# Block 2's feed-forward, first product: seven block products in place of eight for pairs of output blocks

## The chip, the cores and the metric

The kernel runs on one core of one Trainium2 chip. The metric is device time in microseconds (us) of one execution, as a median over several runs. Engines are named as the profile names them: PE is TensorE's matmul, PEld its weight load, DVE is VectorE, ACT is ScalarE, POOL is GpSimd, SP is SyncE, on whose queue the weight loads are issued.

## The reference

Two transformer blocks over 512 tokens of width 1024, in float32. The second has two layers, and each ends in this feed-forward; the change touches nothing else:

```python
D_MODEL = 1024
SEQ = 512
DEPTH_2 = 2
D_FF_2 = 4 * D_MODEL
...
        h = rmsnorm(x, mlp_norm[l])
        u = jnp.square(jax.nn.relu(jnp.einsum('bsd,df->bsf', h, w_ff1[l])))
        x = x + jnp.einsum('bsf,fd->bsd', u, w_ff2[l])
```

## The kernel before

Everything is kept feature-major: a tile has 128 features on its partitions and the 512 tokens along its row. The residual stream is eight such tiles, X0 to X7. To get float32 accuracy from PE's faster fp32r mode, each operand is split into a rounded part (hi, made by an ACT cast) and the rest (lo, made by a DVE subtraction), and each product is three matmuls: hi·hi, lo·hi and hi·lo (`mm3`). A weight block of 128 x 1024 numbers is loaded by one DMA into a raw buffer (`load_w`, a ring of three), then split into a hi and a lo tile (rings of two).

A layer's feed-forward has eight chunks (ch = 0 to 7). A chunk has two stages. Stage ff1 makes four blocks of 128 hidden features: each is 8 contraction steps x 3 = 24 matmuls of 512 columns into a bank of PSUM, and `emit_relu2` then takes it from the bank with DVE (relu and scale), squares it on ACT, and splits it into u hi and lo. Stage ff2 multiplies the four u tiles by four weight blocks; each gives two output tiles of 12 matmuls, which DVE adds to X (`add_residual`, X0 to X7 in order). Both stages take their banks from a ring of two ("mm"), so a group of matmuls cannot begin before DVE has taken the group two before it out of its bank. The 32 blocks that the change speaks of are a layer's 8 chunks x 4 blocks.

Each engine executes its instructions in the order in which they stand in its queue. That order is made when the program is built: a list scheduler goes by priorities, and `tc.high_priority(offset=...)` moves a weight load and its split ahead of other work, by 250 (LOOKAHEAD) before. An instruction that waits holds up all that stand behind it on its engine.

Names in the trace: L0 and L1 are block 2's layers; L1wf_r, L1wf_h and L1wf_l are the raw, hi and lo weight tiles of both stages, L1wf_p their banks, L1m the normed input, L1u the hidden tiles, L1rl the relu tiles, and fin is the last ff2 of the kernel, which `finish` runs in two token halves of 256 columns.

Of the kernel before, what the change touches and what calls it, by code (L numbers as in the profile page):

```python
# [10 lines left out]
F32 = mybir.dt.float32  # L11
F32R = mybir.dt.float32r
# [3 lines left out]
AF = mybir.ActivationFunctionType  # L16
ALU = mybir.AluOpType
# [39 lines left out]
def _f(t):  # L57
    return t.bitcast(F32)
# [125 lines left out]
def transformer_kernel(ctx: ExitStack, tc: tile.TileContext, d, out):  # L184
    nc = tc.nc
# [82 lines left out]
    C = {n: packed[:, c] for n, c in PACK.items()}  # L268
# [69 lines left out]
    def split(x, name):  # L338

        hi, lo = act_pair(name)  # L340
        S.copy(hi, x)
        V.tensor_tensor(lo, x, _f(hi), ALU.subtract)
        return hi, lo

    def normed(gain, name):

        h = []
        for k in range(KT):
            hi, lo = act_pair(f"{name}{k}")
# [13 lines left out]
    def load_w(src, name, tags=None):  # L363

        kt, cols = src.shape[1], src.shape[2]
        n = kt * cols
        raw = early.pop(len(warm), None) if len(warm) < 2 else None
        load = raw is None
        if load:
            raw = wp.tile([P, 1120], F32, tag="raw", name=name + "_r", bufs=3)  # L370
        warm.append(True)
        if tags:
            hi, lo = (pair(t, name + t, F32R).rearrange("p a b -> p (a b)") for t in tags)
        else:
            hi = wp.tile([P, 1120], F32R, tag="hi", name=name + "_h", bufs=2)
            lo = wp.tile([P, 1120], F32R, tag="lo", name=name + "_l", bufs=2)
        clock.take()
        with tc.high_priority(offset=LOOKAHEAD):
            if load:
                nc.sync.dma_start(raw[:, :n], src.rearrange("p k c -> p (k c)"))  # L380
            for c in (slice(0, n),) if load else (slice(0, n // 2), slice(n // 2, n)):
                S.copy(hi[:, c], raw[:, c])  # L382
                V.tensor_tensor(lo[:, c], raw[:, c], _f(hi)[:, c], ALU.subtract)  # L383
        clock.take(background=True)
        return (hi[:, :n].rearrange("p (k c) -> p k c", c=cols), lo[:, :n].rearrange("p (k c) -> p k c", c=cols))

    def mm3(ps, lh, ll, rh, rl, start, stop):
        TE.matmul(ps, lh, rh, start=start, stop=False)  # L388
        TE.matmul(ps, ll, rh, start=False, stop=False)  # L389
        TE.matmul(ps, lh, rl, start=False, stop=stop)  # L390

    def spare(n, name):

        if "s" in pool:
            return [bank("s", f"{name}_{i}") for i in range(n)]
        return [two_banks(f"{name}_{i}")[:, 0] for i in range(n)]

    def gemm_fm(src, h, emit, name, m0=0, banks=()):

        kt, cols = src.shape[2], src.shape[3]  # L400
        banks = list(banks)
        for b in range(src.shape[0]):
            wh, wl = load_w(src[b], f"{name}_{b}")
            for m in range(cols // P):
                ps = banks.pop(0) if banks else bank("mm", f"{name}_p{b}_{m}")
                c = slice(m * P, (m + 1) * P)
                for k in range(kt):
                    mm3(ps, wh[:, k, c], wl[:, k, c], h[k][0], h[k][1], k == 0, k == kt - 1)
                    if k % 2 == 1 and k < kt - 1:
                        yield True  # L410
                emit(m0 + b * (cols // P) + m, ps)
                yield True
# [38 lines left out]
    def run(gen):  # L451
        for _ in gen:
            pass
# [643 lines left out]
    def layer(l):  # L1097
        L = f"L{l}"
        h = normed(C["attn_norm"][:, l * KT : (l + 1) * KT], L + "h")
# [263 lines left out]
        h3 = normed(C["mlp_norm"][:, l * KT : (l + 1) * KT], L + "m")  # L1363
        rn3, rb3 = stats(L + "st3")
        for ch in range(8):
            u = []

            def emit_relu2(m, ps):
                t = sb("evt", f"{L}rl{ch}{m}")
                V.scalar_tensor_tensor(t, ps, 0.0, rb3, ALU.max, ALU.mult)  # L1370
                S.activation(t, t, AF.Square)
                u.append(split(t, f"{L}u{ch}_{m}"))

            run(gemm_fm(d["w_ff1"][l, 4 * ch : 4 * ch + 4], h3, emit_relu2, f"{L}wf1{ch}", 0, spare(2, L + "spf") if ch == 0 else ()))
            if l == 1 and ch == 7:
                finish(d["w_ff2"][l, ch], u)
            else:
                run(gemm_fm(d["w_ff2"][l, ch], u, add_residual, f"{L}wf2{ch}"))

    def finish(src, u):  # L1380

        w = [load_w(src[b], f"wfin{b}", t) for b, t in enumerate((("pa", "pb"),) * 3 + (("qs", "kh"),))]
        for half in range(2):
            t0 = slice(half * 256, (half + 1) * 256)
            for m in range(KT):
                wh, wl = w[m // 2]
                ps = bank("mm", f"fin{half}{m}")[:, :256]
                c = slice(m % 2 * P, (m % 2 + 1) * P)
                for k in range(4):
                    mm3(ps, wh[:, k, c], wl[:, k, c], u[k][0][:, t0], u[k][1][:, t0], k == 0, k == 3)  # L1390
                with tc.high_priority(offset=LOOKAHEAD):
                    V.tensor_tensor(X[m][:, t0], X[m][:, t0], ps, ALU.add)
            acc = sum_squares(f"stf{half}", t0, half == 1)
            pb = spread(inv_rms(acc, f"stf{half}", D), f"stf{half}")[:, :256]
            for k in range(0, KT, 2):
                o = sb("kA" if half == 0 else "kB", f"fo{half}{k}").rearrange("p (a t) -> p a t", a=2)
                for a in range(2):
                    V.scalar_tensor_tensor(o[:, a], X[k + a][:, t0], C["final_norm"][:, k + a : k + a + 1], pb, ALU.mult, ALU.mult)
                nc.sync.dma_start(out[:, k : k + 2, t0], o)

    for l in range(2):
        layer(l)
# [122 lines left out]
```

## Time and profile before

| what | value |
|---|---|
| time, median of 3 runs | 2021.6 us (2020.47 to 2024.03) |
| the profiled execution's own time | 2021.86 us |
| its span, first to last instruction | 2020.1 us |
| PE busy | 1973.4 us, 98% of the span |
| DVE busy | 1175.5 us, 58% |
| ACT busy | 880.0 us, 44% |
| POOL busy | 44.3 us, 2% |
| mean granted TensorE clock | 0.991 of full speed |

PE is busy nearly throughout, and the chain that ended last runs through it. Matmuls overlap one another, so what a matmul costs is the distance from its start to the next one's start, not its own length.

### The profile page before, as it was taken

The page shows a single profiled execution, that of the slowest core. Times are in us where ns is not written, and L with a number is a line of the kernel's source. Part 1 is how long each engine was busy: PE and PEld are TensorE (multiplying, and loading weights), DVE is VectorE, ACT ScalarE, POOL GpSimd, SP SyncE. Part 2 cuts the span into 40 slices and gives each one's busy share as a digit, 9 for nine tenths or more (in the row PEclk, how much of TensorE's full clock was granted, in tenths as well). Part 3 has the DMA queues.
Part 4 walks back from the last instruction along what each step waited for, and adds up shares of the span by engine and source line. Part 5 has one row for each costly group of instructions (what it writes and reads, how often), then busy time and mean ns, then how long its engine had stood idle before and what let it go on. Part 6 is the DMA issues. An engine that isn't in the chain of part 4 may idle for free.

```text
span 2020.1 us, 25945 instructions
## 1 busy us (share of the span) xinstructions
PE 1973.4 (98%) x10197; PEld 1611.3 (80%) x10197; DVE 1175.5 (58%) x2032; ACT 880.0 (44%) x1494; POOL 44.3 (2%) x87
## 2 busy tenths in 40 slices
PE   8999899999999999999999999999999999999998
PEld 7888766788888878787778888888888778888887
DVE  7685877744444457558764444447466864444446
ACT  6642555522222235587542223335577643322223
POOL 0000000000000000001000000000000000000000
PEclk9998999999999999999999999999999999999999
DMA  5222200122222222212122222223221212222222
GB/s 185 72 76 65 69 27 22 53 94 94 94 94 94 95 96 91 83 42 85 61 84 94 94 98 99 95 94 104 75 68 58 74 63 95 98 99 95 94 94 73
DMA packets 50922, 168.65 MB, mean 83 GB/s; under 512 B 5808, under 2 KB 8240, under 8 KB 50800
## 3 DMA queue, kind: packets, MB, share of 16 engines
q1 hardware_dynamic: 47680, 161.93, 23.4%
q0 software_dynamic: 2976, 4.98, 1.2%
q8 instruction: 81, 1.33, 0.3%
q14 instruction: 41, 0.34, 0.1%
q10 hardware_dynamic: 144, 0.07, 0.0%
HBM read 160.14 MB, written 2.10 MB: 80 GB/s over the span
## 4 chain that ended last, share of the span: by engine, by line
PE 49%; ACT 3%; DVE 1%; issue 1%; DVEq 0%; ACTq 0%
PE L0wf_p L390 6%; PE L0wf_p L388 6%; PE L0wf_p L389 6%; PE L1wf_p L390 5%; PE L1wf_p L388 5%; PE L1wf_p L389 5%; PE L1z L1210 1%; PE L0wo_p L388 1%; PE L1wo_p L388 1%; PE L0wo_p L389 1%; PE L1wo_p L389 1%; PE L0wo_p L390 1%; PE L1wo_p L390 1%; PE L1sbo L1224 1%; PE L1wdf_p L388 0%
## 5 line engine op out<-in xcount | busy, mean ns | idle before, releaser
L382 ACT CAST L0wf_h<-L0wf_r 128x1024 fp32r<-128x1024 f32 x64 | 67.3, 1051 | 229.3 <-PE L0wf_p L390 224.8
L382 ACT CAST L1wf_h<-L1wf_r 128x1024 fp32r<-128x1024 f32 x60 | 63.1, 1051 | 221.0 <-PE L1wf_p L390 216.7
L390 PE MATMUL wgu_p<-h_l,wgu_h 128*128 128x512 f32 x328 | 128.8, 393 | 0.0
L388 PE MATMUL wgu_p<-h_h,wgu_h 128*128 128x512 f32 x328 | 128.7, 392 | 0.0
L389 PE MATMUL wgu_p<-h_h,wgu_l 128*128 128x512 f32 x328 | 128.6, 392 | 0.0
L382 ACT CAST wgu_h<-wgu_r 128x1024 fp32r<-128x1024 f32 x44 | 46.2, 1051 | 168.6 <-issue 65.1
L388 PE MATMUL L0wf_p<-L0u_h,L0wf_h 128*128 128x512 f32 x256 | 100.7, 393 | 0.0
L389 PE MATMUL L0wf_p<-L0u_h,L0wf_l 128*128 128x512 f32 x256 | 100.3, 392 | 0.0
L390 PE MATMUL L0wf_p<-L0u_l,L0wf_h 128*128 128x512 f32 x256 | 99.4, 393 | 0.0
L390 PE MATMUL L0wf_p<-L0m_l,L0wf_h 128*128 128x512 f32 x240 | 94.2, 393 | 0.0
L390 PE MATMUL L1wf_p<-L1m_l,L1wf_h 128*128 128x512 f32 x240 | 94.2, 393 | 0.0
L388 PE MATMUL L0wf_p<-L0m_h,L0wf_h 128*128 128x512 f32 x240 | 94.2, 392 | 0.0
L388 PE MATMUL L1wf_p<-L1m_h,L1wf_h 128*128 128x512 f32 x240 | 94.2, 392 | 0.0
L389 PE MATMUL L0wf_p<-L0m_h,L0wf_l 128*128 128x512 f32 x240 | 94.1, 392 | 0.0
L389 PE MATMUL L1wf_p<-L1m_h,L1wf_l 128*128 128x512 f32 x240 | 94.1, 392 | 0.0
L383 DVE TENSOR_TENSOR L0wf_l<-L0wf_r,L0wf_h 128x1024 fp32r<-128x1024 f32 x64 | 78.4, 1225 | 24.6 <-ACT L0wf_h L382 24.6
L388 PE MATMUL L1wf_p<-L1u_h,L1wf_h 128*128 128x512 f32 x224 | 88.1, 393 | 0.0
L389 PE MATMUL L1wf_p<-L1u_h,L1wf_l 128*128 128x512 f32 x224 | 87.8, 392 | 0.0
L383 DVE TENSOR_TENSOR L1wf_l<-L1wf_r,L1wf_h 128x1024 fp32r<-128x1024 f32 x60 | 73.5, 1225 | 23.3 <-ACT L1wf_h L382 23.3
L390 PE MATMUL L1wf_p<-L1u_l,L1wf_h 128*128 128x512 f32 x224 | 87.0, 393 | 0.0
L456 DVE TENSOR_TENSOR X<-X,L0wf_p 128x512 f32<-128x512 f32 x64 | 44.0, 687 | 67.2 <-PE L0wf_p L390 67.2
L456 DVE TENSOR_TENSOR X<-X,L1wf_p 128x512 f32<-128x512 f32 x56 | 38.5, 688 | 66.6 <-PE L1wf_p L390 66.6
(829 smaller groups left out, 5389.9 us busy)
## 6 DMA issues: line engine op xcount, KB each, us to landing
L0wf_r<-w_ff SPq DMA_DIRECT2D x64, 512.0 KB, 3.2
L1wf_r<-w_ff SPq DMA_DIRECT2D x60, 512.0 KB, 3.3
wgu_r<-w_gu SPq DMA_DIRECT2D x44, 512.0 KB, 3.2
wdn_r<-w_dn SPq DMA_DIRECT2D x22, 512.0 KB, 3.3
wns_r<-w_nsa SPq DMA_DIRECT2D x8, 512.0 KB, 3.6
wout_r<-w_out SPq DMA_DIRECT2D x8, 512.0 KB, 3.3
L0wsb_r<-w_sbqk SPq DMA_DIRECT2D x8, 512.0 KB, 3.2
L0wdf_r<-w_dfqk SPq DMA_DIRECT2D x8, 512.0 KB, 3.2
```

Source lines behind the costliest of these rows:

```text
L382: S.copy(hi[:, c], raw[:, c])
L383: V.tensor_tensor(lo[:, c], raw[:, c], _f(hi)[:, c], ALU.subtract)
L388: TE.matmul(ps, lh, rh, start=start, stop=False)
L389: TE.matmul(ps, ll, rh, start=False, stop=False)
L390: TE.matmul(ps, lh, rl, start=False, stop=stop)
L456: V.tensor_tensor(X[m], X[m], ps, ALU.add)
L1210: TE.matmul(ps[:, g, c0:], lhs, rhs[:, g], start=False, stop=(m == len(terms) - 1), skip_group_check=True)
L1224: TE.matmul(po[g * 64 : (g + 1) * 64, j * P + c0 : j * P + c1], sv[j][:, (2 * i + g) * 64 : (2 * i + g + 1) * 64], e[:, g, c0:c1], start=( ...
```

## The change

In each layer, chunk 0 keeps the plain ff1. In chunks 1 to 7 the four blocks are made as two pairs by `gemm_seven`. A pair's product (256 features x 1024 inputs by 1024 inputs x 512 tokens) is cut in two along each of the three directions, and the two-by-two block product is done with seven block products instead of eight, in Strassen's scheme with Winograd's sums. Each of the seven is 128 features x 512 inputs x 256 tokens: 4 contraction steps x 3 = 12 matmuls of 256 columns. So a pair has 84 matmuls of 256 columns where it had 48 of 512.

The scheme needs sums of operands. Weight sums are made for each pair, on POOL: `s1`, `s2`, `a21` (in place) and `s4`, four additions of 128x512. The seven weight operands are then split one by one (`weight_part`: an ACT cast and a DVE subtraction of 128x512 each), where the pair before had two splits of 128x1024. Their tiles come from twelve slots in rotation, so the sixth operand (f) of a pair lies where the first (a) of the pair before it lay. Token sums are made once for each layer from X (`token_parts`), on DVE and ACT, in chunk 0. The seven products (a to g in the order of the program) share three banks; between them ACT copies and DVE additions of 256 columns combine the results (`x`, `y` and `z` are the tiles xy, u0 and u1). `emit_relu2` then works from SBUF.

```diff
+AHEAD7 = 350
...
             def emit_relu2(m, ps):
-                t = sb("evt", f"{L}rl{ch}{m}")
+                t = ps if ch else sb("evt", f"{L}rl{ch}{m}")
                 V.scalar_tensor_tensor(t, ps, 0.0, rb3, ALU.max, ALU.mult)
                 S.activation(t, t, AF.Square)
                 u.append(split(t, f"{L}u{ch}_{m}"))
 
-            run(gemm_fm(d["w_ff1"][l, 4 * ch : 4 * ch + 4], h3, emit_relu2, f"{L}wf1{ch}", 0, spare(2, L + "spf") if ch == 0 else ()))
+            if ch == 0:
+                run(gemm_fm(d["w_ff1"][l, 0:4], h3, emit_relu2, f"{L}wf1{ch}", 0, spare(2, L + "spf")))
+                parts = token_parts(C["mlp_norm"][:, l * KT : (l + 1) * KT], h3, L)
+            else:
+                for n in (0, 2):
+                    gemm_seven(d["w_ff1"][l, 4 * ch + n : 4 * ch + n + 2], parts, lambda m, t: emit_relu2(n + m, t),
+                               f"{L}w7{ch}{n}", "to"[n // 2])
...
+    slots = [("kA",) * 2, ("kB",) * 2, ("kA",) * 2, ("kB",) * 2, ("h1",) * 2, ("h2",) * 2, ("kG",) * 2,
+             ("pa",), ("h0",), ("pa",), ("h0",), ("pa",)]
+    turn_ = [0]
+
+    def weight_part(x, name):
+        s = slots[turn_[0] % len(slots)]
+        turn_[0] += 1
...
+        S.copy(hi, x)
+        V.tensor_tensor(lo, x, _f(hi), ALU.subtract)
...
+    def token_parts(gain, h, name):
...
+        for k in range(4):
...
+            V.tensor_tensor(t1, a[:, two], a[:, one], ALU.subtract)
+            S.activation(t1, t1, AF.Copy, scale=ga)
+            S.activation(t3, a[:, two], AF.Copy, scale=ga)
+            V.scalar_tensor_tensor(t2, c[:, two], gc, t1, ALU.mult, ALU.subtract)
+            V.scalar_tensor_tensor(t3, c[:, two], gc, t3, ALU.mult, ALU.subtract)
+
+            V.scalar_tensor_tensor(t4, c[:, one], gc, t2, ALU.mult, ALU.subtract)
+            for (hi, lo), t in zip(parts, (t1, t2, t3, t4)):
+                S.copy(hi[:, k], t)
+                V.tensor_tensor(lo[:, k], t, _f(hi)[:, k], ALU.subtract)
...
+    def gemm_seven(src, parts, emit, name, third):
+
+        b11, b21, b22, t1, t2, t3, t4 = parts
+        raw = []
+        with tc.high_priority(offset=AHEAD7):
+            for n in range(2):
+                r = wp.tile([P, 1120], F32, tag="raw", name=f"{name}_r{n}", bufs=3)
+                nc.sync.dma_start(r[:, :1024], src[n].rearrange("p k c -> p (k c)"))
+                raw.append(r)
+            a11, a12, a21, a22 = raw[0][:, 0:T], raw[0][:, T : 2 * T], raw[1][:, 0:T], raw[1][:, T : 2 * T]
+            s12 = pair("kx", name + "_s")
+            s1, s2, s4 = s12[:, 0], s12[:, 1], sb("ho", name + "_s4")
+            G.tensor_tensor(s1, a21, a22, ALU.add)
+            G.tensor_tensor(s2, s1, a11, ALU.subtract)
+            G.tensor_tensor(a21, a11, a21, ALU.subtract)
+            G.tensor_tensor(s4, a12, s2, ALU.subtract)
+            order = (("a", a11, b11), ("b", s2, t2), ("c", s1, t1), ("d", a12, b21), ("e", a21, t3), ("f", s4, b22), ("g", a22, t4))
+            w = [weight_part(x, name + e) for e, x, _ in order]
...
+        def product(i, ps, start):
+            (wh, wl), (bh, bl) = w[i], order[i][2]
+            for k in range(4):
+                for m, (x, y) in enumerate(((wh, bh), (wl, bh), (wh, bl))):
+                    TE.matmul(ps, x[:, k], y[k], start=start and k == 0 and m == 0, stop=k == 3 and m == 2, skip_group_check=True)
+
+        p0, p1, p2 = banks
+        xy, u0, u1 = (sb("evt", f"{name}{e}") for e in "xyz")
+        product(0, p0, True)
+        S.copy(xy[:, one], p0)
+        product(1, p1, True)
+        V.tensor_tensor(xy[:, two], p1, xy[:, one], ALU.add)
+        product(2, p2, True)
+        V.tensor_tensor(u1[:, two], p2, xy[:, two], ALU.add)
+        product(3, p0, False)
+        S.copy(u0[:, one], p0)
+        product(4, p1, True)
+        V.tensor_tensor(u1[:, two], p1, u1[:, two], ALU.add)
+        product(5, p2, False)
+        V.tensor_tensor(u0[:, two], p2, xy[:, two], ALU.add)
+        emit(0, u0)
+        product(6, p1, False)
+        V.tensor_tensor(u1[:, one], p1, xy[:, two], ALU.add)
+        emit(1, u1)
```

The change adds a line at the top, so a line of the helpers above it stands one lower after it (`add_residual` is L456 before and L457 after).

DVE in the ff2 stage of layer 0's chunk 3, where its second and third weight blocks are worked on. Before, each X addition stands right behind the one before it or one split:

```order
L456 TENSOR_TENSOR X2_98<-X2_98,L0wf23_p1_0_9875 128x512
L456 TENSOR_TENSOR X3_99<-X3_99,L0wf23_p1_1_9889 128x512
L383 TENSOR_TENSOR L0wf23_3_l_9939<-L0wf23_3_r_9937,L0wf23_3_h_9938 128x1024
L456 TENSOR_TENSOR X4_100<-X4_100,L0wf23_p2_0_9909 128x512
L456 TENSOR_TENSOR X5_101<-X5_101,L0wf23_p2_1_9923 128x512
L383 TENSOR_TENSOR L0wf14_0_l_9973<-L0wf14_0_r_9971,L0wf14_0_h_9972 128x1024
```

The same place in the changed program. L0w740 is layer 0, chunk 4, the pair that begins with block 0; the letter behind is the operand (a to g), r0 and r1 are the two raw tiles, s the sums s1 and s2, s4 the last sum:

```order
L457 TENSOR_TENSOR X3_99<-X3_99,L0wf23_p1_1_10366 128x512
L384 TENSOR_TENSOR L0wf23_3_l_10416<-L0wf23_3_r_10414,L0wf23_3_h_10415 128x1024
L1402 TENSOR_TENSOR L0w740b_10462<-L0w740_s_10452,L0w740b_10462 128x512
L1402 TENSOR_TENSOR L0w740c_10465<-L0w740_s_10452,L0w740c_10465 128x512
L1402 TENSOR_TENSOR L0w740d_10468<-L0w740_r0_10448,L0w740d_10468 128x512
L1402 TENSOR_TENSOR L0w740e_10471<-L0w740_r1_10450,L0w740e_10471 128x512
L1402 TENSOR_TENSOR L0w740f_10474<-L0w740_s4_10453,L0w740f_10474 128x512
L1402 TENSOR_TENSOR L0w740gl_10478<-L0w740_r1_10450,L0w740gh_10477 128x512
L457 TENSOR_TENSOR X4_100<-X4_100,L0wf23_p2_0_10386 128x512
L1402 TENSOR_TENSOR L0w742al_10600<-L0w742_r0_10589,L0w742ah_10599 128x512
L1402 TENSOR_TENSOR L0w742dl_10612<-L0w742_r0_10589,L0w742dh_10611 128x512
L457 TENSOR_TENSOR X5_101<-X5_101,L0wf23_p2_1_10400 128x512
```

Six subtractions of the next pair's operands now stand ahead of the X4 addition. The second place is the end of the same ff2 stage and the first products of chunk 4. ACT there, in the changed program:

```order
L1401 CAST L0w742eh_10615<-L0w742_r1_10591 128x512
L1401 CAST L0w742fh_10619<-L0w742_s4_10594 128x512
L383 CAST L0wf24_0_h_10735<-L0wf24_0_r_10734 128x1024
L1462 COPY L0w740x_10483<-L0w740_p_10481 128x256
L383 CAST L0wf24_1_h_10769<-L0wf24_1_r_10768 128x1024
L1401 CAST L0w742g_10623<-L0w742_r1_10591 128x512
```

And DVE at that place; the last row combines product c, and the tile `q` is the bank that product f then adds to:

```order
L457 TENSOR_TENSOR X6_102<-X6_102,L0wf23_p3_0_10420 128x512
L384 TENSOR_TENSOR L0wf24_0_l_10736<-L0wf24_0_r_10734,L0wf24_0_h_10735 128x1024
L457 TENSOR_TENSOR X7_103<-X7_103,L0wf23_p3_1_10434 128x512
L1402 TENSOR_TENSOR L0w742fl_10620<-L0w742_s4_10594,L0w742fh_10619 128x512
L384 TENSOR_TENSOR L0wf24_1_l_10770<-L0wf24_1_r_10768,L0wf24_1_h_10769 128x1024
L1464 TENSOR_TENSOR L0w740x_10483<-L0w740_p_10481,L0w740x_10483 128x256
L1402 TENSOR_TENSOR L0w742g_10623<-L0w742_r1_10591,L0w742g_10623 128x512
L1466 TENSOR_TENSOR L0w740z_10485<-L0w740_q_10482,L0w740x_10483 128x256
```

The additions that free the banks of the first products stand behind splits of the second pair and of the next ff2 weights. On PE the scheduler has also moved the first pair's product a, up to its last matmul, ahead of the ff2 group p3_0; the last matmul of it stands behind p3_1.

## Rows read from the trace of the kernel before

**Rows 1.** The page: span and part 1, busy time and share of each engine.
```profile
span 2020.1 us, 25945 instructions
...
PE 1973.4 (98%) x10197; PEld 1611.3 (80%) x10197; DVE 1175.5 (58%) x2032; ACT 880.0 (44%) x1494; POOL 44.3 (2%) x87
```

**Rows 2.** Busy time in one chunk of layer 1: PE, PEld, DVE, ACT, POOL, clock, DMA.
```profile
1722.00:1766.00 44.00, 44.00 (x192) 35.77 (x191) 20.44 (x25) 13.02 (x16) 0.00 (x0) 1.00 0.28 96
```

**Rows 3.** Timeline of layer 1's feed-forward: start us, length us, engine, line [idle before, releaser].
```profile
1901.73 1.05 ACT L382 CAST L1wf_h<-L1wf_r 128x1024 fp32r<-128x1024 f32 x1 [3.41 <-PE L1wf_p L390]
1902.81 1.22 DVE L383 TENSOR_TENSOR L1wf_l<-L1wf_r,L1wf_h 128x1024 fp32r<-128x1024 f32 x1 [0.39 <-ACT L1wf_h L382]
1904.06 5.78 SPq L380 DMA_DIRECT2D L1wf_r<-w_ff  x2
...
1907.18 1.05 ACT L382 CAST L1wf_h<-L1wf_r 128x1024 fp32r<-128x1024 f32 x1 [4.40 <-PE L1wf_p L390]
...
1929.27 1.05 ACT L382 CAST L1wf_h<-L1wf_r 128x1024 fp32r<-128x1024 f32 x1 [3.22 <-PE L1wf_p L390]
...
1934.86 1.05 ACT L382 CAST L1wf_h<-L1wf_r 128x1024 fp32r<-128x1024 f32 x1 [3.35 <-PE L1wf_p L390]
```

**Rows 4.** Timeline of PE in fin: the first and last of 84 matmuls of 256 columns.
```profile
1988.24 0.38 PE L388 MATMUL fin<-L1u_h,wfin1pa 128*128 128x256 f32 x1 [0.40 <-DVE X L1392]
...
1998.29 0.28 PE L390 MATMUL fin<-L1u_l,wfin0pa 128*128 128x256 f32 x1
```

**Rows 5.** Groups by line and form, DVE and ACT: count | busy us, mean ns | idle before.
```profile
L342 DVE TENSOR_TENSOR L0u_l<-L0rl,L0u_h 128x512 fp32r<-128x512 f32 x32 | 22.2, 693 | 0.0
...
L383 DVE TENSOR_TENSOR L0wf_l<-L0wf_r,L0wf_h 128x1024 fp32r<-128x1024 f32 x64 | 78.4, 1225 | 24.6 <-ACT L0wf_h L382 24.6
...
L1392 DVE TENSOR_TENSOR X<-X,fin 128x256 f32<-128x256 f32 x16 | 6.6, 419 | 2.3 <-PE fin L390 1.7
...
L341 ACT CAST L0u_h<-L0rl 128x512 fp32r<-128x512 f32 x32 | 19.9, 622 | 1.0
...
L320 ACT ACTIVATE stf_sq<-X 128x256 f32<-128x256 f32 x14 | 5.8, 418 | 14.6 <-DVE X L1392 13.3 <-DVE stf_acc L323 1.3
```

**Rows 6.** Timeline of DVE: two independent additions back to back.
```profile
965.26 0.69 DVE L1155 TENSOR_TENSOR L0rt<-L0wdf_p,L0cr 128x512 f32<-128x512 f32 x1 [0.52 <-ACT L0rr L1153]
965.87 0.68 DVE L1156 TENSOR_TENSOR L0rr<-L0rr,L0sr 128x512 f32<-128x512 f32 x1
```

**Rows 7.** The page's part 6: weight loads, KB each, median us to landing.
```profile
L0wf_r<-w_ff SPq DMA_DIRECT2D x64, 512.0 KB, 3.2
```

**Rows 8.** All of POOL's casts (L548): shortest, median and longest ns, starts, forms.
```profile
L548 POOL CAST lev_mask<-lm x5: 608/708/1052, 17.3 to 21.3; 128x512 uint8<-128x512 f32 x4, 128x256 uint8<-128x256 f32 x1
```

**Rows 9.** Timeline of POOL: its last two casts together, and the second alone.
```profile
20.61 1.51 POOL L548 CAST lev_mask<-lm 128x512 uint8<-128x512 f32 x2 [1.16 <-DMA lm<-lev_mask]
...
21.27 0.85 POOL L548 CAST lev_mask<-lm 128x256 uint8<-128x256 f32 x1
```

**Rows 10.** Timeline of DVE at the same place, and the same operations without POOL.
```profile
14.79 0.68 DVE L323 TENSOR_TENSOR st_acc<-st_acc,st_sq 128x512 f32<-128x512 f32 x1
15.39 0.15 DVE L553 TENSOR_TENSOR lbm<-packed 128x4 f32<-128x4 f32 x1
...
20.76 1.10 DVE L323 TENSOR_TENSOR st_acc<-st_acc,st_sq 128x512 f32<-128x512 f32 x1
21.78 0.35 DVE L558 TENSOR_TENSOR lbs<-lbe 128x4 f32<-128x4 f32 x1
```

**Rows 11.** Busy time by stretch around a wait of PE; the clock is third from the end.
```profile
1003.50:1006.70 3.20, 0.16 (x2) 0.00 (x0) 1.99 (x10) 0.78 (x4) 0.00 (x0) 0.98 0.00 0
1006.70:1010.10 3.40, 2.47 (x7) 1.88 (x8) 0.76 (x2) 0.69 (x1) 0.00 (x0) 0.50 0.02 5
1010.10:1013.50 3.40, 3.05 (x8) 1.90 (x7) 2.02 (x3) 1.82 (x3) 0.00 (x0) 0.52 0.00 0
```

More of the change, by code (lines that the diff above doesn't have):

```diff
@@ L1378, in layer @@
                 run(gemm_fm(d["w_ff2"][l, ch], u, add_residual, f"{L}wf2{ch}"))
+    slots = [("kA",) * 2, ("kB",) * 2, ("kA",) * 2, ("kB",) * 2, ("h1",) * 2, ("h2",) * 2, ("kG",) * 2,
[4 more added lines that the diff above has]
+        turn_[0] += 1
+        if len(s) == 1:
+            t = pair(s[0], name, F32R)
+            hi, lo = t[:, 0], t[:, 1]
+        else:
+            hi, lo = (pool["gp"].tile([P, T], F32R, tag=g, name=name + e, bufs=rings[g]) for g, e in zip(s, "hl"))
+        S.copy(hi, x)
+        V.tensor_tensor(lo, x, _f(hi), ALU.subtract)
+        return [z.rearrange("p (k c) -> p k c", c=P) for z in (hi, lo)]
@@ new lines, in token_parts @@
+    def token_parts(gain, h, name):
+        one, two = slice(0, T // 2), slice(T // 2, T)
+        tags = ("qs", "kh", "kl", "pb")
+        parts = [[pair(g, f"{name}T{g}{e}", F32R).rearrange("p a (b t) -> p (a b) t", t=T // 2) for e in "hl"] for g in tags]
+        for k in range(4):
+            a, c = X[k], X[k + 4]
+            ga, gc = gain[:, k : k + 1], gain[:, k + 4 : k + 5]
+            w = sb("evt", f"{name}w{k}")
+            w2 = sb("evt", f"{name}v{k}")
+            t1, t2, t3, t4 = w[:, one], w[:, two], w2[:, one], w2[:, two]
+            V.tensor_tensor(t1, a[:, two], a[:, one], ALU.subtract)
[7 more added lines that the diff above has]
+                V.tensor_tensor(lo[:, k], t, _f(hi)[:, k], ALU.subtract)
+        b11 = [[h[k][e][:, one] for k in range(4)] for e in range(2)]
+        b21 = [[h[k + 4][e][:, one] for k in range(4)] for e in range(2)]
+        b22 = [[h[k + 4][e][:, two] for k in range(4)] for e in range(2)]
+        return [b11, b21, b22] + [[[z[:, k] for k in range(4)] for z in p] for p in parts]
@@ new lines, in gemm_seven @@
+    def gemm_seven(src, parts, emit, name, third):
[15 more added lines that the diff above has]
+            w = [weight_part(x, name + e) for e, x, _ in order]
+        one, two = slice(0, T // 2), slice(T // 2, T)
+        pp = pool["p"].tile([P, 2, T], F32, tag="b", name=name + "_p")
+        banks = [pp[:, 0, one], pp[:, 1, one], bank(third, name + "_q")[:, one]]
+        def product(i, ps, start):
[21 more added lines that the diff above has]
+        emit(1, u1)
```

## The prediction

> **What bounds the kernel now.** I read the page first: PE is busy 98% of the span, POOL 2% [rows 1]. Then busy time by stretch, one chunk of a feed-forward at a time: PE is busy in all 44.00 us at full clock, DVE in 20.44, ACT in 13.02, POOL not at all [rows 2]. So in these stages PE sets the pace, and DVE and ACT wait for it: their splits end waits of 3 to 4 us for PE [rows 3]. What counts is then PE's matmul spacing, and whether the other engines can keep ahead of PE once they have more to do.
>
> Spacing comes from starts that PE releases. In ff2 two casts released by PE, 24 matmuls apart, start at 1901.73 and 1907.18: 5.45/24 = 0.227 us for 512 columns. In ff1 they start at 1929.27 and 1934.86: 5.59/24 = 0.233 [rows 3]. For 256 columns with the same three-matmul pattern, fin shows 84 matmuls, as many as a pair now has, from 1988.24 to 1998.29: 10.05/83 = 0.121 [rows 4].
>
> **What PE saves.** A chunk's ff1 was 96 x 0.233 = 22.36 us; it becomes 2 x 84 x 0.121 = 20.33. The saving is 2.0 us a chunk, 14 chunks: 28 us. It is less than the eighth of the columns (2.8 us a chunk), since 0.121 is more than half of 0.233. Weight loads grow from 48 to 84 a pair; in fin they stood beside 256-column matmuls at that spacing, so they are in the price. Break-even is 2.0 us of new PE waiting a chunk.
>
> **What the others gain in work.** A 128x512 DVE operation takes 0.69 us until its result is seen, and 0.61 from start to start [rows 6]; a 128x1024 split 1.22, a 256-column one 0.42; an ACT cast of 512 takes 0.62, of 1024 1.05 [rows 3, 5], and 256 columns 0.42 [rows 5]. In a chunk DVE loses four 1.22 splits and four relu operations of 0.69, and gains 14 operand splits and four relu operations of 0.69 and ten additions of 0.42: 20.4 - 4.9 + 9.7 + 4.2 = 29.4 us of some 42. ACT goes from 13.0 to 13.0 - 4.2 + 14 x 0.62 + 4 x 0.42 = 19.2. Both would fit on average. POOL gets eight additions a chunk.
>
> What an addition of two 128x512 operands costs on POOL no row shows. The nearest is its cast of one such operand, 0.61 us at the shortest [rows 8]. I bound it by 0.61 below (a second operand costs nothing) and 1.2 above (it costs as much again), and take 0.9, the middle, since nothing in the trace says which end is nearer. As a price from the Trainium skill alone: "GPSIMD Engine Reference", the section on performance versus the Vector engine, has 4497 ns for 2048 columns, an estimate of 1.1 us for 512, by which the sum below would come to some 2095; no row here shows it.
>
> POOL and DVE hinder each other. At 20.76 a DVE addition with both inputs in SBUF took 1.10 us instead of 0.68, and one of four columns at 21.78 took 0.35 instead of 0.15 [rows 10]. POOL's casts ran from 20.61 to 21.27 and 21.27 to 22.12 [rows 9]. The long addition ends at 21.86, 0.59 after the first cast; the half-size cast, which took longer than a full one, ends 0.26 after that; the small addition ends with it, at 22.13. Each waited for the one that had come first. The Trainium skill states this as a rule ("SBUF — State Buffer", the section on SBUF's two separate sides): a DVE operation with two SBUF inputs and a GpSimd operation that reads SBUF exclude each other for the whole instruction. These rows agree. It speaks against this change, which puts 8 POOL additions among DVE's splits. I take additions to X, with one input in PSUM, as not held up; no row shows it.
>
> **The first wait: X4.** I count from the first matmul of an ff2 stage (layer 0, chunk 3 into 4). Its blocks end at 5.5, 10.9 and 16.35 (24 x 0.227 each). The third block's cast can start only when PE frees the first block's hi tile, as in [rows 3]: 5.5 to 6.55; its DVE split runs 6.6 to 7.8 and frees the raw buffer for r1 of pair 740. The load is issued 0.03 later, as at 1904.06 [rows 3], and lands after 3.2 us [rows 7]: 11.05. Only now can POOL begin, s1 first, then s2, then e, then s4. DVE has the split of the fourth ff2 block (wanted at 12.05), then b, which needs s2 cast by ACT. Taken in turn at 0.9: s1 11.1-12.0, s2 12.05-12.95, the split 12.95-14.15, e 14.15-15.05, b 15.05-15.75, s4 15.7-16.6; c starts at 16.6, d 17.2, e 17.85, f 18.45, g 19.05, and X4 19.65 to 20.35. But X4 must empty the bank that PE's group p3_0 uses. PE wants it at 16.35 + 11 x 0.121 (product a, moved there as cover) = 17.7. **PE waits 2.7 us.** With 0.61 the same sequence gives X4 done at 19.25 and 1.55 us; with 1.2, 21.55 and 3.85.
>
> **The second wait: z.** p3_1 then ends at 20.4 + 5.45 = 25.85; call it T. r0 of 740 is free when d's split is done at 17.9, so r1 of 742 lands at 21.15. POOL, again in turn with DVE: s1 21.55-22.45, s2 22.5-23.4, e 24.1-25.0, s4 25.7-26.6. Operand f of 742 lies where 740's a lay, so its cast needs PE's last a matmul, which stands behind p3_1 (T + 0.35), and s4: 26.65-27.3. Queued behind it on ACT are ff2's next first split, 27.3-28.3, and the copy of a, to 28.7. The second of these weight blocks needs r0 of 742 free (s4, 26.6), so it lands at 29.85 and is cast by 30.95. DVE in its order: first split to 29.55, X7 to 30.2, f to 30.8, second split 31.0-32.2, x 32.15-32.55, g 32.5-33.2, z 33.55. Product f may add to its bank only after z. PE gets there after the last a, c, b, d and four matmuls of the next a: T + 41 x 0.121, with some 0.1 of start-up, = 30.75. **PE waits 2.8 us.** Other chunks have another order (five of them with z ahead of g, one with z ahead of the split), so I take 2.3 as the mean; with 0.61 1.5, with 1.2 3.0.
>
> Later additions are on time by the same count (742's own z at 42.7, where PE wants it at 43.4), and the wait of the next ff2 for u stays at the few tenths that it was.
>
> **The sum.** A chunk: 2.7 + 2.3 - 2.0 = +3.0 us, 14 chunks: +42. Token sums: 4 x (5 x 0.42 + 3 x 0.47) = 14 us of DVE a layer in chunk 0, whose cover is DVE's idle 44 - 20.4 = 23.6 us; with the first two pairs' splits (9.7) and POOL's turns (7.2) the demand is 51 of 44, so 0 to 7 us a layer, and I take 3.5: +7. `finish` wants the token sums' buffers for its lo weights, free only after the last product: one to two splits of 1.22, +2. Against the profiled execution's 2021.9 (median of the runs 2021.6): 2021.9 + 42 + 7 + 2 = **2073 us**. With POOL at 0.61 and no cost in chunk 0: 1.55 + 1.5 - 2.0 = 1.05 a chunk, 2037. With 1.2: 4.85 x 14 = 68, 14 and 3: 2107.
>
> **Rivals.**
> *The work is hidden: faster.* If POOL and DVE did not wait for each other here and an addition took 0.61, s4 would be done at 13.7, the six splits would start at 13.3 and X4 be done at 17.65, ahead of PE's 17.7; z would be late by about 1.0 us in the mean. -1.0 x 14 and up to 5 for chunk 0 and the end: some 2010; with z on time too, 1994. For it: both engines have idle time on average. Against it: [rows 9, 10], and the late landing of r1. It decides at 2.0 us of waits a chunk.
> *The clock falls.* PE waited 3.2 us at 1003.5, and the next 6.8 us ran at 0.50 of the clock [rows 11], the 1.2 GHz level. Two waits of 2 to 4 us a chunk are near that. Half clock costs 1.7 us per 3.4; once a chunk, over 3.4 or 6.8 us, 14 x 1.7 to 3.4 = 24 to 48 on top: 2097 to 2121. Against: the waits of 2.7 and 2.3 are shorter.
> *Nothing moves.* Waits of 1.5 to 2.5 us a chunk eat the saving: 2015 to 2029.
>
> **Chances.** My sum (2037 to 2107) 0.50; hidden 0.24; clock falls 0.14; near break-even 0.12, of which 0.07 within 0.2% (about 4 us, what a measurement tells from no change), 0.01 faster and 0.04 slower. So faster 0.25, same 0.07, slower 0.68. The range runs from 2006, well into the hidden case, to 2112; outside are fully hidden work and the worse half of the clock's case. My sum's own range is 2037 to 2107.
>
> **What would show it.** Right: 256-column matmuls at 0.12; in each ff2 a PE wait of 2 to 4 us at p3_0 with an X addition as releaser; a second, released by DVE's z, at product f; L1402 subtractions over 0.69 us in the mean where POOL runs; POOL additions of 0.6 to 1.2 us. Wrong: no idle time of PE at p3_0, or DVE durations unchanged beside POOL (then the hidden case), or granted clock below 1.00 in these chunks.

## The result, and the profile after

The changed kernel takes 2147.4 us (median of 4 runs, 2142.8 to 2151.4); the kernel before, on the same chip, 2021.5. The ratio is 1.0621, with an interval of 1.0608 to 1.0634: slower, as forecast, but 126 us slower instead of 51, and beyond the range. The profiled execution has a span of 2142.7 us, 122.6 more than before.

The head of its page, which answers to [rows 1]: PE is no longer busy all the time, and no other engine is.

```profile
span 2142.7 us, 28834 instructions
PE 2002.7 (93%) x11205; PEld 1665.9 (78%) x11205; DVE 1365.7 (64%) x2376; ACT 974.6 (45%) x1738; POOL 223.6 (10%) x199
```

A window over five chunks of layer 0, from the end of chunk 1's last addition to X to that of chunk 6, first of the kernel before, then of the changed one. Columns: the window, its length, busy time (and number of instructions) of PE, weight loads, DVE, ACT and POOL, then the granted clock, the DMA share and GB/s.

```profile
1120.10:1341.30 221.20, 221.20 (x962) 179.81 (x961) 103.38 (x121) 65.12 (x81) 0.00 (x0) 1.00 0.28 96
```
```profile
1141.70:1400.00 258.30, 228.17 (x1328) 197.94 (x1327) 162.79 (x223) 93.25 (x152) 63.44 (x42) 0.96 0.24 82
```

A chunk took 221.2/5 = 44.2 us and takes 51.7. The two bounds also show the first chunks: chunk 1 ends 21.6 us later than before. In layer 1 the same ends were 1742.0 and 1963.1 and are 1826.9 and 2082.8. So ten chunks in mid-course cost 37.1 + 34.8 = 72 us, the two first chunks of both layers 21.6 + 30.3 = 52 us, and the remaining last chunks and the end come to -1.

What PE waits for, in layer 0 from 1200 to 1400 (engine, tile and line of the waiting matmul, its releaser, us in total, times, longest):

```profile
PE L0wf_p L389 <- DVE X L457: 14.7, 4, 3.9
PE L0w_p L1457 <- ACT L0w760x L1462: 3.1, 1, 3.1
PE L0w_p L1457 <- ACT L0w750x L1462: 2.2, 1, 2.2
```

The first is the predicted wait of p3_0 for X4, once a chunk and 3.7 us long. The chain behind it is the predicted one. POOL's four additions for pair 740, then DVE's subtractions up to X4 (start, us, engine, line):

```profile
1224.35 1.29 POOL L1443 TENSOR_TENSOR L0w_s<-L0w_r 128x512 f32<-128x512 f32 x1 [33.89 <-DMA L0w_r<-w_ff]
1225.73 2.15 POOL L1444 TENSOR_TENSOR L0w_s<-L0w_s,L0w_r 128x512 f32<-128x512 f32 x1
1227.84 1.30 POOL L1445 TENSOR_TENSOR L0w_r<-L0w_r,L0w_r 128x512 f32<-128x512 f32 x1
1229.10 1.75 POOL L1446 TENSOR_TENSOR L0w_s<-L0w_r,L0w_s 128x512 f32<-128x512 f32 x1
```
```profile
1224.13 0.69 DVE L457 TENSOR_TENSOR X<-X,L0wf_p 128x512 f32<-128x512 f32 x1 [2.04 <-PE L0wf_p L391]
1225.21 1.51 DVE L384 TENSOR_TENSOR L0wf_l<-L0wf_r,L0wf_h 128x1024 fp32r<-128x1024 f32 x1 [0.39 <-ACT L0wf_h L383]
1228.57 1.12 DVE L1402 TENSOR_TENSOR L0w740b<-L0w_s,L0w740b 128x512 fp32r<-128x512 f32 x1 [1.84 <-ACT L0w740b L1401]
1229.61 1.79 DVE L1402 TENSOR_TENSOR L0w740c<-L0w_s,L0w740c 128x512 fp32r<-128x512 f32 x1
1231.32 0.68 DVE L1402 TENSOR_TENSOR L0w740d<-L0w_r,L0w740d 128x512 fp32r<-128x512 f32 x1
...
1233.73 0.67 DVE L457 TENSOR_TENSOR X<-X,L0wf_p 128x512 f32<-128x512 f32 x1
```

s1 waits for the landing of r1. From there to the end of s4 it is 6.5 us; the forecast had 5.5 (11.1 to 16.6). The shortest addition is 1.29; s2 takes 2.15, while DVE's split (1225.21 to 1226.72) runs in its first microsecond. In turn, c's subtraction takes 1.79 and ends 0.55 after s4; alone, d's takes 0.68. This is the taking of turns of [rows 9, 10]. The X addition at 1224.13, with one input in PSUM, overlaps s1 and still takes 0.69: it is not held up, as I had assumed without a row.

Two windows around X4, columns as above: PE's idle stretch, and 3.4 us soon after it.

```profile
1230.70:1234.40 3.70, 0.28 (x3) 0.07 (x1) 3.70 (x7) 2.18 (x4) 0.15 (x1) 1.00 0.35 128
1235.60:1239.00 3.40, 3.40 (x10) 2.66 (x9) 2.04 (x4) 1.24 (x2) 3.32 (x3) 0.51 0.29 114
```

The wait has a price beside its length: behind it the granted clock is 0.51, the lower of the two levels, for 3.4 us, which loses another 1.7 (an estimate, 3.4 x 0.49).

### The profile page after: what moved, and what is told of

The parts are those of the page before. It is cut to its first block, busy times and chain, and to the rows that moved or that the text cites. A ratio compares the mean times of both kernels' runs of the same rounds, so it can differ in the third digit from the quotient of the medians.

```text
span 2142.7 us, 28834 instructions
## 1 busy us (share of the span) xinstructions
PE 2002.7 (93%) x11205; PEld 1665.9 (78%) x11205; DVE 1365.7 (64%) x2376; ACT 974.6 (45%) x1738; POOL 223.6 (10%) x199
## 5 line engine op out<-in xcount | busy, mean ns | idle before, releaser
L389 PEld LDWEIGHTS L0wf_p<-L0u_h,L0wf_h 128*128 128x128 f32 x256 | 51.5, 201 | 38.7 <-issue 22.8
L383 ACT CAST L0wf_h<-L0wf_r 128x1024 fp32r<-128x1024 f32 x36 | 37.8, 1049 | 81.0 <-PE L0wf_p L391 63.2
L389 PEld LDWEIGHTS L1wf_p<-L1u_h,L1wf_h 128*128 128x128 f32 x224 | 45.4, 203 | 36.3 <-issue 18.7
L390 PEld LDWEIGHTS wgu_p<-h_h,wgu_l 128*128 128x128 f32 x328 | 61.8, 188 | 13.9
L391 PEld LDWEIGHTS wgu_p<-h_l,wgu_h 128*128 128x128 f32 x328 | 61.7, 188 | 13.7
L389 PEld LDWEIGHTS wgu_p<-h_h,wgu_h 128*128 128x128 f32 x328 | 61.7, 188 | 13.7
L383 ACT CAST L1wf_h<-L1wf_r 128x1024 fp32r<-128x1024 f32 x32 | 33.6, 1049 | 84.4 <-PE L1wf_p L391 68.2
L389 PE MATMUL wdn_p<-u_h,wdn_h 128*128 128x512 f32 x176 | 69.8, 399 | 1.4 <-ACT u_h L342 0.7
L391 PE MATMUL wdn_p<-u_l,wdn_h 128*128 128x512 f32 x176 | 69.1, 394 | 0.0
L390 PE MATMUL wdn_p<-u_h,wdn_l 128*128 128x512 f32 x176 | 68.2, 392 | 0.0
L457 DVE TENSOR_TENSOR X<-X,wdn_p 128x512 f32<-128x512 f32 x48 | 32.8, 687 | 47.0 <-PE wdn_p L391 47.0
L457 DVE TENSOR_TENSOR X<-X,L0wf_p 128x512 f32<-128x512 f32 x64 | 43.3, 682 | 29.8 <-PE L0wf_p L391 29.8
```

The costliest lines, as they stand in the source:

```text
L457: V.tensor_tensor(X[m], X[m], ps, ALU.add)
```

## The experiments

Times are of one execution each, beside the kernel before on the same chip (2020.2 to 2022.8), unless said otherwise. The us a chunk are from the same five-chunk window. Where it holds more or fewer matmuls than five chunks have (264 a chunk with two pairs), because products are drawn ahead, 0.124 us a matmul (worked out below) corrects it; the changed kernel's 51.7 becomes 51.5. The four executions of the changed kernel lie up to 8.5 us apart, 0.6 us a chunk if spread over 14, so single runs that differ by less are not told apart.

**What do POOL's sums cost in all?** The four additions are left out, and parts are made from the raw blocks:

```diff
-            G.tensor_tensor(s1, a21, a22, ALU.add)
...
-            G.tensor_tensor(s4, a12, s2, ALU.subtract)
+            order = (("a", a11, b11), ("b", a11, t2), ("c", a21, t1), ("d", a12, b21), ("e", a21, t3), ("f", a12, b22), ("g", a22, t4))
```

> Left out: the four POOL additions of each pair; parts b, c, e and f are cast and subtracted from the raw weight blocks themselves, so every other instruction stays and the output is not the reference's. Theory A (the loss hangs on the chain of POOL's additions: X4 stands on DVE behind six subtractions, and these wait for POOL; the clock falls behind that wait): the wait of some 3.75 us before p3_0 goes, the stretch of 3.4 us at half clock (1.5 us a chunk) goes with it, and product waits of 2.4 us a chunk shrink to under 0.5; a chunk falls from 51.2 to 43 or 44 us, chunks 0 and 1 keep some 5 us a layer; 2143 less 12 x 7 and 2 x 15: some 2030, between 2000 and 2050. Theory C (the token sums and the first pair cost most): 2100 or more, since they are untouched.

2037.5 us, as theory A has it; theory C falls as the main cause.

```profile
1136.60:1348.90 212.30, 212.21 (x1298) 187.61 (x1297) 137.99 (x219) 88.98 (x150) 0.00 (x0) 1.00 0.27 95
```

PE is busy throughout and the clock stays up; corrected for 22 matmuls, a chunk takes 43.0 us. So the products save 1.2 us a chunk when nothing is late, not 2.0.

**Is it X4's place?** Only the priority of the additions to X changes:

```diff
-        V.tensor_tensor(X[m], X[m], ps, ALU.add)
+        with tc.high_priority(offset=AHEAD7 + 250):
+            V.tensor_tensor(X[m], X[m], ps, ALU.add)
```

> Only the order changes: the additions to X get a higher priority than the operands of the coming pair, so that on DVE X4 stands directly behind part b and not behind f and g. Theory A: X4 no longer waits for POOL's fourth addition and four more subtractions; the wait before p3_0 falls from 3.75 us to under 1, the half clock behind it goes (1.5 us a chunk), the operands come up to 0.7 us later and product waits may grow by as much: 5 us less in 12 chunks, 2070 to 2105. Theory B (POOL and DVE hinder each other, wherever X stands): 2130 to 2145.

2140.9 us, where theory B had it; theory A falls in this form. The same stretch of PE's waits now reads:

```profile
PE L0w_p L1458 <- ACT L0w760x L1463: 6.2, 1, 6.2
PE L0wf_p L389 <- DVE X L458: 4.1, 7, 0.7
PE L0w_p L1458 <- ACT L0w740x L1463: 3.2, 1, 3.2
```

The waits for X shrank to 0.7 at most, as intended, and PE waits up to 6.2 us at product b instead; a chunk still takes 51.1. So X4's wait was only the place where PE met a supply of parts that takes 51 us a chunk.

**Is it that the parts wait for the sums?** POOL still adds, but the parts come from the raw blocks:

```diff
-            G.tensor_tensor(a21, a11, a21, ALU.subtract)
+            G.tensor_tensor(s1, a11, a21, ALU.subtract)
```

(and `order` as in the run without sums)

> Left out: the use of POOL's sums. POOL does the same four additions on the same inputs into the same tiles (the third one into another), but no part is made of them: b, c, e and f come from the raw blocks. The output is not the reference's. Theory A (the chain: DVE's and ACT's queues wait for the sums): close to the run without sums, 2030 to 2060, with DVE's subtractions still stretched to about 1.1 us in the mean beside POOL. Theory B (POOL's and DVE's hindering of each other by itself takes the time, whoever waits for the sums): 2110 to 2140, waits before p3_0 stay over 3 us.

2143.4 us, 50.9 a chunk, although no part waits for a sum:

```profile
1147.20:1401.90 254.70, 229.97 (x1321) 200.23 (x1321) 173.68 (x220) 89.23 (x150) 65.42 (x42) 0.95 0.24 82
```

The 0.6 us a chunk less is no more than executions differ, and it is a net figure: DVE is busy 34.7 us a chunk here and 32.6 in the changed kernel, so its operations now meet POOL's more. (The waits at p3_0 are shorter than theory B had them, at most 2.6 us.) Two things are left that POOL does: it hinders DVE, and it holds the raw buffers until its last addition. The loads show the second: in the changed kernel's five chunks, five of them wait for that addition (engine, line, releaser, us in total, times, longest):

```profile
SPq L1438 <- POOL L0w_s L1446: 19.0, 2, 9.5
SPq L381 <- POOL L0w_s L1446: 17.6, 3, 5.9
```

The next run keeps the hindering and takes away most of the holding: only s1 reads a raw block, the other three a table that stays in SBUF.

```diff
+            G.tensor_tensor(s1, a21, cos_t, ALU.add)
+            G.tensor_tensor(s2, s1, cos_t, ALU.subtract)
+            G.tensor_tensor(s1, cos_t, s1, ALU.subtract)
+            G.tensor_tensor(s4, cos_t, s2, ALU.subtract)
```

> Left out: POOL's use of the weights and the use of its sums. POOL does four additions of the same size per pair, started by the landing of r1 as before (its first one reads one half of r1), the others on a table that lies in SBUF all the time, and no part is made of them; so DVE and ACT wait for no sum, and the raw buffers are not held by POOL's second to fourth addition. The output is not the reference's. The two earlier runs left two theories. Theory B (POOL and DVE hinder each other by running at the same time, whoever uses the sums): DVE's subtractions still 1.0 to 1.2 us in the mean, 2110 to 2145. Theory D (the raw buffers are held until POOL's last addition, so the next loads start late): 2035 to 2070.

2092.5 us, between the two: 47.4 us a chunk, and no load waits for POOL any more.

```profile
1141.80:1376.30 234.50, 219.12 (x1298) 191.27 (x1297) 164.11 (x219) 89.17 (x149) 66.11 (x42) 0.98 0.24 86
```

Both hold. From no additions (43.0) to additions that hold next to nothing is 4.4 us a chunk. From there to the run before it is 50.9 - 47.4 = 3.5, which I put down to holding the raw buffers; but DVE lost 2 us a chunk more to POOL there (34.7 against 32.8), so part of the 3.5 may be hindering. The changed kernel itself is the cleaner partner: DVE is as busy in it (32.6), so I put the 51.5 - 47.4 = 4.1 between the two down to holding and waiting for sums together, and not to DVE time. Layer 1's five chunks give the same picture (43.3, 46.9, 51.1 and 51.6: steps of 3.6, 4.2 and 0.5). The other way round, r1 gets buffers of its own in the real kernel:

```diff
-                r = wp.tile([P, 1120], F32, tag="raw", name=f"{name}_r{n}", bufs=3)
+                r = pair("h0", f"{name}_r1").rearrange("p a b -> p (a b)") if n else wp.tile([P, 1120], F32, tag="raw", name=f"{name}_r0", bufs=3)
...
-             ("pa",), ("h0",), ("pa",), ("h0",), ("pa",)]
+             ("pa",), ("pa",), ("pa",)]
```

> As the changed kernel, with its sums on POOL, but the second raw block of a pair (r1) lands in two buffers of its own (the pair buffers h0), so that its load waits for no split of ff2; the operand parts have ten places in turn in place of twelve. Theory D (the raw ring of three, held until POOL's last addition, delays the loads): s1 starts several us sooner, a chunk takes 45.5 to 48 us in place of 51.2, 2070 to 2110. Theory B (POOL and DVE hinder each other, and that alone): 2130 to 2150.

2110.3 us, 48.0 a chunk, at the upper edge of theory D:

```profile
1147.30:1386.20 238.90, 223.48 (x1311) 194.86 (x1310) 166.14 (x221) 91.20 (x150) 61.92 (x41) 0.97 0.24 84
```

That is 3.5 less than the changed kernel (4.2 in layer 1), about the same amount. It is not quite the same thing: r1's load no longer waits for a split of ff2 either, and there are two places fewer for the parts.

**What does the hindering cost by itself?** In the kernel before, with its plain products, POOL adds a table to each relu result, twice a block:

```diff
                 u.append(split(t, f"{L}u{ch}_{m}"))
+                for q in range(2):
+                    s = sb("ho", f"{L}pool{ch}{m}{q}")
+                    G.tensor_tensor(s, t, cos_t, ALU.add)
```

> The kernel before, all products plain, plus eight POOL additions of 128x512 a chunk in all 16 chunks (two behind each relu result, added to a table, the sums unused). No weight buffer is held by POOL. Theory B taken as a matter of time on DVE alone: DVE's splits get longer where POOL runs (over 1.22 us in the mean), but DVE is busy in 20 of 44 us, so PE hardly waits: 2022 to 2030. If a POOL addition costs PE time wherever it runs: 16 x 2 us or more, over 2050.

2040.1 us beside 2020.2, between my two expectations: 45.3 us a chunk, 1.1 more than plain.

```profile
1122.90:1349.30 226.40, 222.40 (x961) 179.80 (x960) 124.24 (x120) 65.18 (x81) 66.99 (x40) 1.00 0.27 93
```

DVE's split of u by groups, and PE's waits in the whole span:

```profile
L342 DVE TENSOR_TENSOR L0u_l<-L0rl,L0u_h 128x512 fp32r<-128x512 f32 x25 | 43.4, 1736 | 0.2 <-ACT L0u_h L341 0.2
```
```profile
PE L0wf_p L390 <- DVE L0u_l L342: 6.4, 8, 0.8
```

The split meets POOL's first addition and takes 1.74 instead of 0.69 us [rows 5]. Where PE wants that u next, at the head of ff2, it waits, once a chunk. DVE had idle time; that didn't help the one operation that was wanted at once.

**Would DVE do the sums better?** In the four additions:

```diff
-            G.tensor_tensor(s1, a21, a22, ALU.add)
+            V.tensor_tensor(s1, a21, a22, ALU.add)
...
```

> The four additions of a pair move from POOL to DVE, 8 x 0.68 us a chunk more on DVE, one after the other, and no wait of POOL and DVE for each other. Theory A (late r1 and a long chain ahead of X4): the chain stays but its additions take 0.61 to 0.68 us in place of 1.3 to 2.1, so X4 comes about 2 us sooner: wait before p3_0 of 1.5 to 2.5 us, clock mostly up, a chunk of 46 to 48 us: 2060 to 2100. Theory B (the hindering alone): 2030 to 2060. If DVE's load itself is the limit: 2140 or more.

2073.1 us, 46.0 a chunk and no half clock in the five-chunk window:

```profile
1141.70:1369.30 227.60, 216.26 (x1302) 188.80 (x1301) 161.39 (x260) 90.03 (x148) 1.62 (x3) 1.00 0.27 92
```

DVE did some forty additions more than in the changed kernel's window, and its busy time for five chunks did not rise (162.79 there): what it had lost to waiting for POOL was as much as doing POOL's work itself. So the 5.5 us a chunk between the two kernels are not DVE's load; with POOL the same work is done later. PE still waits, up to 2.3 us at product d, as DVE's splits of the second pair and of the next ff2 weights stand ahead of the first pair's x.

**Chunk 0.** The token sums alone, all products plain:

```diff
-                    gemm_seven(d["w_ff1"][l, 4 * ch + n : 4 * ch + n + 2], parts, lambda m, t: emit_relu2(n + m, t),
...
+                run(gemm_fm(d["w_ff1"][l, 4 * ch : 4 * ch + 4], h3, emit_relu2, f"{L}wf1{ch}"))
```

> Left out: the seven products. All 32 blocks take the plain path as before the change, and only the token sums are computed in chunk 0 and not used; the output is the reference's. It prices the token sums alone. My prediction's term (7 us for both layers, from 0 to 14): 2022 to 2036, 2029 taken. Theory C (that the token sums cost the most of chunk 0's 22 and 27 us): 2045 to 2070.

2036.6 us beside 2022.8: 14 us, 7.3 in layer 0's chunk 0 and 7.2 in layer 1's, the upper bound of my term.

```profile
PE L0wf_p L389 <- DVE X L457: 5.2, 2, 3.7
PE L1wf_p L389 <- DVE X L457: 5.1, 2, 3.7
```
```profile
1056.00:1067.00 11.00, 5.85 (x24) 4.00 (x23) 11.00 (x28) 7.84 (x20) 0.00 (x0) 1.00 0.28 96
```

The additions to X must wait until the token sums have read X; DVE works the 11 us through without a break, and PE stands for 5.2 of them. DVE's idle time of that chunk lies elsewhere (it is busy 3.1 of the 8.0 us from 1040 on, 3.3 of the 8.2 from 1075 on). So the sums were put there, a quarter behind each block of the first product:

```diff
                 u.append(split(t, f"{L}u{ch}_{m}"))
+                if ch == 0:
+                    token_step(tt, C["mlp_norm"][:, l * KT : (l + 1) * KT], m, L)
```

First with the sums on DVE and both pairs:

> As the run with sums on DVE (2073), and the token sums are computed one quarter behind each of the four blocks of chunk 0's first product, 5.5 us apart, in place of all four at its end beside the first additions to X, which must wait for them. If chunk 0's loss comes from that crowding: 10 to 25 us less, 2048 to 2063. If it comes from the first pair's products being drawn ahead into chunk 0: 2070 to 2075.

2043.5 us: 29.6 less than without the spread, more than I expected of the crowding; what else it took away was not looked into. With the sums on POOL, as in the changed kernel:

> As the changed kernel (2147), sums on POOL, and only the token sums are computed one quarter behind each block of chunk 0's first product. Chunk 0 and the start of chunk 1 lost 22 and 27 us there, of which the token sums by themselves are 7.3 a layer (the run with token sums alone). If the token sums' crowding of DVE is what also makes the first pair's operands late: 25 to 35 us less, 2112 to 2122. If POOL's additions for the first pair are the larger part: about 14 less, 2130 to 2138.

2129.0: 18 us less, between the two readings and nearer to the second. Chunk 1 of layer 0 still ends at 1133.4, 13.3 later than before, and the same stretch of layer 1 is 21.1 longer; with neither POOL's additions nor the crowding:

> Left out: the four sums of a pair, parts b, c, e and f come from the raw blocks; the output is not the reference's. Token sums spread. It bounds what seven products could bring if sums of weights were free: chunks of 42.6 us as in the first run without sums, chunk 0 without its 17 us a layer: 2000 to 2012. If chunk 0's loss there came from the first pair and not from the token sums: 2030 to 2037.

2020.2 beside 2020.2, where I expected 2000 to 2012; the two stretches are 1.5 and 2.7 us longer than before. So of the 52 us of the first chunks some 18 go with the token sums' place and then 30 with POOL's additions. The order counts: with POOL's additions taken away first (the first run without sums, whose two stretches are 16.5 and 15.2 longer than before) it is 20 for them and 27.5 for the place, so part of the loss needs both. And with both pairs, a kernel that gets its weight sums for nothing only breaks even. Its window has 43.4 us a chunk (218.0 us, 1329 matmuls), so the chunks did not keep the 43.0 of the first run without sums; why, I can't say.

**A version that gains.** One pair a chunk by seven products, the other two blocks plain, sums on DVE, token sums spread:

```diff
+                run(gemm_fm(d["w_ff1"][l, 4 * ch : 4 * ch + 2], h3, emit_relu2, f"{L}wf1{ch}"))
+                gemm_seven(d["w_ff1"][l, 4 * ch + 2 : 4 * ch + 4], parts, lambda m, t: emit_relu2(2 + m, t), f"{L}w7{ch}2", "o")
```

> As the run before it, but only the second two of the four blocks of a chunk go by seven products, the first two by the plain path. DVE's extra work halves (about 30 of 44 us busy), and so does the saving: 1.0 us a chunk, 14 us in all. If DVE's queue is what makes PE wait, the waits go and a chunk takes 43.3 to 44 us: 2015 to 2030 with chunk 0's cost. If any pair brings a wait of 2 us whatever the load: 2040 to 2060.

2022.3 us: no waits in mid-course, 43.7 us a chunk, but 7 us lost from the last addition of chunk 6 to the end (64.2 us, before 57.0). With `G.` for `V.` in the four additions, on POOL again:

> As the run with one pair a chunk and spread token sums (2022.3), but with the pair's four sums on POOL again. If a POOL addition costs DVE more than an addition of its own (1.3 us of mutual exclusion against 0.61), yet half the load leaves room: a few tenths to 2 us a chunk, 2025 to 2050. If POOL's help is worth anything at this load: under 2022.

2044.2 us, 45.2 a chunk: even at half the load POOL costs 1.5 us more a chunk than DVE. With DVE's sums, and block 2's last chunk plain:

```diff
+            elif (l, ch) == (1, 7):
+                run(gemm_fm(d["w_ff1"][l, 4 * ch : 4 * ch + 4], h3, emit_relu2, f"{L}wf1{ch}"))
```

> As the run with one pair a chunk, sums on DVE and spread token sums (2022.3), but block 2's last chunk takes the plain path in all four blocks, so that the buffers in which the final product's lo weights land are free before that chunk ends. There the run lost 7 us against the kernel before; the plain chunk gives up 0.6. Expected 2014 to 2018, faster than before by some 0.3%. If the loss at the end has another cause: 2022.

2015.1 us (6 runs) against 2021.2 (9 runs): ratio 0.997, interval 0.9958 to 0.9983. That is 0.3%, small but clear of no change, so this beats both kernels. In its profiled execution, the longest of the six (2020.2), the stretch after chunk 6 is 56.9 again, and PE is busy in the whole window:

```profile
1123.50:1341.60 218.10, 218.10 (x1141) 184.65 (x1140) 133.23 (x191) 78.11 (x116) 0.00 (x0) 1.00 0.28 97
```

The spacing follows from it. Before, 221.2/960 = 0.2304 a matmul of 512 columns. Here five chunks have 720 of these and 420 of 256: (218.1 - 720 x 0.2304)/420 = 0.124. A pair saves (221.2 - 218.1)/5 = 0.62 us.

Both pairs with r1 in buffers of its own, sums on DVE, did not work:

> As the run with both pairs, sums on DVE and spread token sums (2043.5), with r1 in the two buffers of its own. If late landings keep DVE's queue full ahead of the x and z additions (there the wait is 2.3 us a chunk): a chunk falls to 43 to 44.5 us, 2015 to 2030. If DVE's load itself makes the wait: 2040 to 2045.

2054.0 us, 11 more than without, outside both expectations, although a chunk took 45.3 us, no more. The loss lies outside that window: 5 us in layer 0's first two chunks, 3 in layer 1's five, 2 at the end. Whether the two places fewer for the parts cause it wasn't tried, and two single runs stand against each other here.

## Why the prediction was wrong in size

- **What bounds it, and the two waits: right.** p3_0 waits for X4, which stands on DVE behind six subtractions and a POOL chain that starts with the late r1. I had 2.7 us and it is 3.7; with my upper bound of the addition the same count gave 3.85. Products wait too, up to 3.1 us and 2.4 a chunk in the mean, close to the 2.3 that I had taken; but the profile names a copy or x at product b or d, not z at product f, so that size is luck. (A slip in that count: PE comes to product f at 25.85 + 41 x 0.121 + 0.1 = 30.9, not 30.75.)
- **The sum of a chunk, +3.0, is +7.3.** By the five-chunk row PE is idle 30.1 of 258.3 us, 6.0 a chunk, where I had 5.0. It is busy 45.4 a chunk, 2.4 more than in the run without sums, where I had nothing; the granted clock of 0.96 explains some 2.1 of that (an estimate, 0.04 x 51.7). The saving is 1.2 and not 2.0. So the largest part of the miss is the clock, and by my count it hangs on the next step.
- **The failed step: "take 0.9, the middle" for a POOL addition.** It takes 1.29 alone and 1.3 to 2.15 in turn with DVE, above my upper bound. By my own count that makes X4's wait 1 us longer, and it took away the reason for leaving the clock out of the sum, that the waits are shorter than 3.2 us. (That the clock would have stayed up behind a wait of 2.7 us no run shows.) The estimate by the Trainium skill ("GPSIMD Engine Reference", performance versus the Vector engine), 1.1, was nearer than my middle, and still short. Its rule of exclusion ("SBUF — State Buffer", SBUF's two separate sides) agrees with the rows shown here.
- **Without a price of its own: how long POOL holds the raw buffers.** I followed when r0 and r1 come free, but treated each wait as an event in one chunk. The run with X moved ahead shows that what counts is the rate of supply: holding the buffers is worth about 3.5 us a chunk, additions at the same time as DVE 4.4. The steps 43.0 + 4.4 + 3.5 + 0.6 = 51.5 are differences of runs and add up by construction; what speaks for the 3.5 independently is the run with r1 in buffers of its own.
- **The saving: 1.2 us a chunk, not 2.0.** The 0.233 for 512 columns came from one interval; the mean of 960 is 0.2304. The 0.121 for 256 columns is 0.124 in the full window of the version that gains. Over 14 chunks that is 17 us instead of 28.
- **The clock was a rival and should have been a term.** I gave "the clock falls" 0.14 because my waits were under 3.2 us. X4's is longer, and the clock falls behind it; in the five chunks it is 0.96 in the mean, which I had named as a sign of being wrong. Its price in that rival, 1.7 to 3.4 us a chunk, holds. The rival "hidden" falls.
- **Chunk 0, the second failed step: 7 us.** The first two chunks of both layers lose 52, some 37 beyond the 2 x 7.3 of two ordinary chunks. The token sums alone take 14. I set DVE's idle time of a whole chunk against the work; as the program placed it, the work could only lie between the last block of ff1 and the first addition to X, which overwrites what it reads. And the first pair's parts and POOL's additions for them, which I had only as a part of DVE's demand, come at the same time; 20 to 30 of the 52 go with these additions.
- **The end: 2 us.** Not measured by itself: the stretch behind chunk 6, chunk 7 included, is 2.9 us longer.

Not settled: how much of the 3.5 us for the held buffers is the clock's fall (the mean clock is 0.95 in the run that holds them and 0.98 in the one that doesn't), how much the waits themselves, and how much DVE's longer hindering; nothing was run that parts them.

## What to carry to other kernels

Giving two-input elementwise work to POOL relieves DVE only if DVE has no operation with two SBUF inputs meanwhile: here eight POOL additions a chunk raised DVE's own busy time from 27.6 us (without sums) to 32.6, 0.6 each, and DVE would have done each in 0.61; and they came later. When an engine waits at one place in each round, move that place first by order alone; if the wait turns up elsewhere and the round takes as long, the limit is a rate, and buffers' holding times are the next thing to read. Idle time is cover only where the work may lie: look for what overwrites its inputs.

## What the hardware showed that I had not expected

A POOL addition of two 128x512 operands needs 1.29 us when DVE does not hold it up, twice its cast's 0.61 [rows 8]. After a PE wait of 3.7 us the clock was 0.51 for 3.4 us. In the run with additions on a table, two stretches of 3.2 and 3.1 us with PE almost idle were followed by 3.5 us at 0.58 and 3.4 us at 0.69 in the mean:

```profile
1158.20:1161.40 3.20, 0.34 (x2) 0.00 (x0) 3.10 (x4) 0.29 (x1) 2.33 (x2) 1.00 0.30 88
1161.50:1165.00 3.50, 3.50 (x15) 3.21 (x16) 1.70 (x3) 2.00 (x4) 0.00 (x0) 0.58 0.15 60
...
1205.40:1208.50 3.10, 0.36 (x2) 0.00 (x0) 3.00 (x4) 0.27 (x1) 2.25 (x2) 1.00 0.30 112
1208.60:1212.00 3.40, 3.40 (x16) 3.03 (x17) 2.11 (x4) 2.81 (x6) 0.00 (x0) 0.69 0.13 47
```
